# Both parts of a weight unit in one tile, 64 bytes beside a multiple of 128

## The chip, the cores and the metric

The kernel runs on one core of a Trainium2 chip. The metric is the device time of one execution in microseconds (us). Before the change it is 2307.37 us, the median of 3 runs (2305.29 to 2307.74).

## What is computed

Two transformer blocks in sequence, both on one sequence of 256 tokens of width 1024, all in float32. The first has two layers: a mixer (an mLSTM group with neighbourhood attention in the one, differential attention in the other), cross attention to 256 memory tokens, and a SwiGLU network with 2816 hidden units. The second has two layers of a SwiGLU network, a mixer of three gated branches (sparse latent attention with a top-64 choice, stick-breaking attention, a short convolution), cross attention, and another SwiGLU network. After each sublayer stands a layer norm over a scaled residual:

```python
def swiglu(x, w_gu, w_down):
    gate, up = jnp.split(x @ w_gu, 2, axis=-1)
    return (jax.nn.silu(gate) * up) @ w_down
...
    x = layer_norm(DEEPNORM_ALPHA * x + ff, ln_g[layer, 2], ln_b[layer, 2])
```

With 256 tokens, nearly all arithmetic is in products of the activations with weight matrices, each weight being used once. The differential attention needs one scalar that the change touches:

```python
    lam = jnp.exp(jnp.sum(lp[0] * lp[1])) - jnp.exp(jnp.sum(lp[2] * lp[3])) + lam_init
    ...
        a = p[:, :, 0] - lam * p[:, :, 1]
```

## The kernel before

**Weight units.** Every weight matrix is cut on the host into units of 128 partitions x 1024 columns of float32 (512 KB), 725 of them (the memory tokens are cut in the same way). The class Stream (line 190) holds the list of units in the order of their use, recorded by a first pass over the program without instructions. Its method _load (line 203) starts a unit's transfer into one of 4 staging tiles `w`, on SyncE's queue. Its method _split (line 211) makes two tiles of it: `hi`, the unit rounded to fp32r by ScalarE (L218), and `lo`, what the rounding left out, by VectorE (L219; put off by `due`, so that it is issued a little later, by `_low`). Up to 10 units are held split at a time, each part in one of the 10 places of its tag in the pool `wp`. pump (line 233) runs loads and splits ahead of use; get (line 248) hands a unit out, and done gives its place free.

**Products.** Activations are split in the same way: `xT` (hi and lo, feature by token), or `ph` and `pl` for computed operands. A float32 product is then three fp32r matmuls added up in PSUM: hi x hi, lo x hi, hi x lo. In unit_group (line 339) the weights are the stationary operand, in slices of 128 columns, and xT streams with 256 columns (L348, L350, L352: 3232 of each). mm3 (line 304, its matmuls L307 to L309) is used by all others: bg_mm, where a unit of the down or output projection streams with 512 or 256 columns against stationary `ph` and `pl`; vproj and vproj_first, where a unit streams with 512 columns against slices of xT; the first two units of each SwiGLU network; the branch products of the mixer; and in mem_open kv_k and kv_v, where both operands are units: the memory tokens, two units held through the whole of it, and the weights. Only the gates of the mLSTM (e_g) have a stationary operand of 64 columns.

**Order.** Instructions are issued in the order of the program, each engine has its own queue, and waits between engines follow from which tile places are written and read. Attention and other small work is written as generators (`bgs`), stepped between units by tick, so that TensorE does it between units. Small products there (L727, L747, L965, L1354 and others) are of plain float32, and the transposes (L551, L646) too; their operands lie in the pools `a1` (places of 1,024 bytes) and `a2` (its widest tile, `av`, is 128 x 4 x 129 float32, 2,064 bytes, and places are kept at multiples of 32 bytes). The pools follow one another in a partition's memory: `one`, `stage`, `wp`, `a1`, `a2` and two small ones.

**Lambda.** tables (line 1466) computes minus lambda for all partitions: a subtraction of the two exponentials, a subtraction of lambda's constant, and a matmul with a row of ones (`onerow`), which spreads it over 128 partitions. build sets `onerow` and `negone` (a 128 x 128 tile of -1, used by the stick-breaking attention) by memsets at the start.

Of the kernel before, what the change touches and what calls it, by code (L numbers as in the profile page):

```python
# [9 lines left out]
F32 = mybir.dt.float32  # L10
F32R = mybir.dt.float32r
AF = mybir.ActivationFunctionType
OP = mybir.AluOpType
# [8 lines left out]
LAM_INIT = 0.8 - 0.6 * math.exp(-0.3)  # L22
# [145 lines left out]

class Blank:


# [16 lines left out]
class Stream:  # L190
# [20 lines left out]
    def _split(self):  # L211
        n = self.net
        cols = self.plan[self.split][2]
        w = self.stage.pop(self.split)
        hi = n.wp.tile([128, 1024], F32R, tag="wh", name="wh")
        lo = n.wp.tile([128, 1024], F32R, tag="wl", name="wl")
        self._low()
        n.nc.scalar.copy(hi[:, :cols], w[:, :cols])  # L218
        self.due = lambda: n.nc.vector.tensor_sub(lo[:, :cols], w[:, :cols], hi[:, :cols].bitcast(F32))  # L219
        self.parts[self.split] = (hi, lo)  # L220
        self.split += 1
        self.live += 1
# [44 lines left out]
class Net:  # L267
# [1198 lines left out]
    def tables(self):  # L1466
        nc, sg, nlam, lp = self.nc, self.sg, self.nlam, self.lp
        nc.vector.tensor_scalar(sg, sg, 1.0 - LAM_INIT, None, op0=OP.mult)

        l2 = self.small.tile([1, 2], F32, tag="l2", name="l2")  # L1470
        pr = self.k1(shape=[1, 64], name="lpr")
        for i in range(2):
            nc.vector.tensor_mul(pr, lp[:, 128 * i:128 * i + 64], lp[:, 128 * i + 64:128 * i + 128])
            nc.vector.reduce_sum(l2[:, i:i + 1], pr, axis=AX.X)
        nc.scalar.activation(l2, l2, AF.Exp)
        nl = self.small.tile([1, 1], F32, tag="l1", name="l1")
        nc.vector.tensor_sub(nl, l2[:, 1:2], l2[:, 0:1])
        nc.vector.tensor_scalar(nl, nl, LAM_INIT, None, op0=OP.subtract)
        for _ in range(4):
            yield  # L1480
        self.rel_table()
        ps = self.bank([128, 1])
        nc.tensor.matmul(ps, self.onerow, nl, start=True, stop=True)
        nc.vector.tensor_copy(nlam, ps)

    def rel_load(self):
# [7 lines left out]
    def build(self):  # L1494
        nc, tc = self.nc, self.tc
        with ExitStack() as ctx:
            pool = lambda name, bufs, **k: ctx.enter_context(tc.tile_pool(name=name, bufs=bufs, **k))
            self.one = pool("one", 1)
            self.stage = pool("stage", STAGE)
            self.wp = pool("wp", W_SLOTS)  # L1500
            self.act = Multi(pool("a1", 35), pool("a2", 18)) if self.real else Blank()
            self.small = SmallMix(pool("sm_col", 24), pool("sm_o", 2)) if self.real else Blank()
            self.psum = pool("psum", 8, space=bass.MemoryType.PSUM)
            self.dram = pool("dram", 1, space=bass.MemoryType.DRAM)
            ctx.enter_context(tc.manual_schedule())
            sq = self.one.tile([128, 3, 128], F32, name="sq")
            self.xT = [self.one.tile([128, 8, S], F32R, tag=f"xT{i}", name="xT") for i in range(2)]
            xq = [self.k2(name="xq") for _ in range(4)]
            for u in range(4):
                nc.scalar.dma_start(xq[u], self.a["xT"][u // 2, :, (u % 2) * 512:(u % 2) * 512 + 512]  # L1510
                                    .rearrange("p (k c) -> p k c", k=2))
            self.xq = xq
            self.ws.start()
            nc.sync.dma_start(sq, self.a["c_sq"])
            self.ident, self.negt, self.strict = (sq[:, i, :] for i in range(3))
            self.mhalf = self.one.tile([128, 8], F32, name="mhalf")
            nc.vector.memset(self.mhalf, -0.5)
            self.negone = self.one.tile([128, 128], F32, name="negone")
            nc.vector.memset(self.negone, -1.0)
            self.onerow = self.one.tile([1, 128], F32, name="onerow")  # L1520
            nc.vector.memset(self.onerow, 1.0)

            subs = [self.even,
                    lambda: self.xattn("x0", "memT", 2, 1),
                    lambda: self.ffn("f0", 2, 2 * ALPHA, 4 * EPS),
                    self.odd,
                    lambda: self.xattn("x1", "memT", 2, 4),
                    lambda: self.ffn("f1", 5, 2 * ALPHA, 4 * EPS)]
            for l in range(2):
                b = 6 + 4 * l  # L1530
                subs += [lambda l=l, b=b: self.ffn(f"h{l}0", b, 4 * ALPHA, 16 * EPS),
                         lambda l=l, b=b: self.mixer(l, b + 1),
                         lambda l=l, b=b: self.xattn(f"y{l}", "memT2", 1, b + 2),
                         lambda l=l, b=b: self.ffn(f"h{l}1", b + 3, 4 * ALPHA, 16 * EPS)]
            if self.start:
                for u in range(4):
                    self.x_split(u)
                self.late_loads()
                self.lam_load()
                self.rel_load()  # L1540
                for _ in self.tables():
                    pass
            for f in subs[self.start:self.stop]:
                f()
            if self.stop < 14:
                self.flush()
                for t in range(2):
                    nc.sync.dma_start(self.out[0, t * 128:t * 128 + 128, :], self.x[:, t, :])
# [40 lines left out]
```

## Time and profile before

| | before |
|---|---|
| median of 3 runs | 2307.37 us |
| profiled execution's own time | 2310.04 us |
| its span | 2308.3 us |
| TensorE (PE) busy | 2277.5 us |
| weight loads (PEld) busy | 2139.0 us |
| VectorE (DVE) busy | 1498.5 us |
| ScalarE (ACT) busy | 1156.3 us |
| GpSimd (POOL) busy | 201.9 us |
| moved from HBM | 403.76 MB, 175 GB/s over the span |
| granted TensorE clock, mean | 0.996 |

Busy times are unions: a matmul's recorded duration of some 0.28 us runs from its start to the modelled end of its way through the array, and several overlap, so that the distance from one start to the next tells the pace and not the duration. A weight load (PEld) runs beside the matmul before its own. Names such as `wh` and `wl` are the program's tiles, with numbers left out; L218 is line 218 of the kernel.

### The profile page before, as it was taken

The numbers are of one execution on the slowest core, as the hardware profiler recorded it, in microseconds if no ns is written. First come the engines' busy times: TensorE is split into PE (matmuls) and PEld (weight loads), VectorE is DVE, ScalarE is ACT, GpSimd is POOL, SyncE is SP. The second block draws the span as 40 slices with busy tenths as digits, with TensorE's granted clock in tenths as the row PEclk, the third lists the DMA queues.
The fourth block names the chain that finished last, engine by engine and source line by source line (L and its number), as shares of the span: only waits on it lengthen the run. The fifth ranks groups of instructions, "written<-read, shape, count | busy, mean of one in ns | idle before, by whom it ended". The sixth has DMA issues, their size and how long they took to land.

```text
span 2308.3 us, 40983 instructions
## 1 busy us (share of the span) xinstructions
PE 2277.5 (99%) x16600; PEld 2139.0 (93%) x16600; DVE 1498.5 (65%) x2271; ACT 1156.3 (50%) x1856; POOL 201.9 (9%) x239
## 2 busy tenths in 40 slices
PE   8999999999999999999999999999999999999998
PEld 6989999998999999999899999999999999999998
DVE  4885665676657557556586677557656576677655
ACT  5555454377435444444745554444443845445542
POOL 0720000011000000000202000000000101100000
PEclk9999999999999999999999999999999999999999
DMA  7644475463437555654364555654753445454752
GB/s 232 164 165 165 158 249 183 146 210 138 161 131 248 183 182 179 207 182 159 116 188 142 202 174 191 210 191 138 238 191 130 165 150 170 162 195 163 248 183 74
DMA packets 118081, 407.50 MB, mean 177 GB/s; under 512 B 14169, under 2 KB 19419, under 8 KB 117891
## 3 DMA queue, kind: packets, MB, share of 16 engines
q1 hardware_dynamic: 116258, 402.00, 52.2%
q0 software_dynamic: 768, 1.57, 0.8%
q8 instruction: 130, 2.13, 0.4%
q10 hardware_dynamic: 864, 1.31, 0.2%
q14 instruction: 61, 0.49, 0.1%
HBM read 403.76 MB, written 1.06 MB: 175 GB/s over the span
## 4 chain that ended last, share of the span: by engine, by line
PE 95%; ACT 2%; DVE 2%; DMA 1%; POOL 0%; issue 0%; ACTq 0%; DVEq 0%; POOLq 0%
PE ps L348 17%; PE ps L350 16%; PE ps L352 16%; PE acc L307 7%; PE acc L308 7%; PE acc L309 7%; PE ps L307 5%; PE ps L309 5%; PE ps L308 5%; PE ps L551 1%; PE ps L727 1%; PE ps L747 1%; DMA xq<-in_xT 1%; PE ps L646 1%; DVE x L536 0%; PE ps L1145 0%
## 5 line engine op out<-in xcount | busy, mean ns | idle before, releaser
L219 DVE TENSOR_TENSOR wl<-w,wh 128x1024 fp32r<-128x1024 f32 x725 | 884.3, 1239 | 378.0 <-ACT wh L218 374.9
L348 PE MATMUL ps<-xT,wh 128*128 128x256 f32 x3232 | 921.5, 285 | 0.0
L350 PE MATMUL ps<-xT,wl 128*128 128x256 f32 x3232 | 914.6, 283 | 0.0
L352 PE MATMUL ps<-xT,wh 128*128 128x256 f32 x3232 | 914.3, 283 | 0.0
L218 ACT CAST wh<-w 128x1024 fp32r<-128x1024 f32 x725 | 747.5, 1050 | 233.3 <-PE ps L352 134.6
L348 PEld LDWEIGHTS ps<-xT,wh 128*128 128x128 f32 x3232 | 619.8, 192 | 10.0 <-issue 5.5
L350 PEld LDWEIGHTS ps<-xT,wl 128*128 128x128 f32 x3232 | 620.0, 192 | 0.6
L352 PEld LDWEIGHTS ps<-xT,wh 128*128 128x128 f32 x3232 | 620.0, 192 | 0.0
L307 PE MATMUL acc<-wh,ph 128*128 128x512 f32 (+1 forms) x940 | 329.2, 350 | 0.6 <-ACT ph L295 0.6
L308 PE MATMUL acc<-wl,ph 128*128 128x512 f32 (+1 forms) x940 | 327.2, 348 | 0.0
L309 PE MATMUL acc<-wh,pl 128*128 128x512 f32 (+1 forms) x940 | 326.0, 347 | 0.0
L307 PEld LDWEIGHTS acc<-wh,ph 128*128 128x128 f32 x940 | 177.9, 189 | 24.9 <-ACT ph L295 0.8
L309 PEld LDWEIGHTS acc<-wh,pl 128*128 128x128 f32 x940 | 177.5, 189 | 23.2 <-DVE pl L296 0.2
L308 PEld LDWEIGHTS acc<-wl,ph 128*128 128x128 f32 x940 | 178.0, 189 | 22.3
L522 POOL TENSOR_TENSOR col<-col,mhalf 128x1 f32<-128x1 f32 (+1 forms) x38 | 28.6, 752 | 1596.7 <-DVE col L530 1521.4
L563 ACT ACTIVATE k<-ps 128x256 f32<-128x256 f32 x120 | 46.0, 383 | 179.2 <-PE ps L352 179.2
L292 ACT CAST ph<-k 128x256 fp32r<-128x256 f32 x120 | 48.8, 407 | 128.7 <-DVE k L565 128.7
L307 PE MATMUL ps<-wh,xT 128*128 128x256 f32 (+1 forms) x304 | 103.9, 342 | 9.4 <-ACT wh L218 9.4
L307 PE MATMUL ps<-wh 128*128 128x256 f32 x384 | 112.6, 293 | 0.0
L564 DVE SCALAR_TENSOR_TENSOR k<-k,ps 128x256 f32<-128x256 f32 x120 | 50.4, 420 | 93.9 <-ACT k L563 93.8
L309 PE MATMUL ps<-wh,wl 128*128 128x256 f32 x384 | 108.6, 283 | 0.0
L308 PE MATMUL ps<-wl,wh 128*128 128x256 f32 x384 | 108.5, 282 | 0.0
(266 smaller groups left out, 2502.1 us busy)
## 6 DMA issues: line engine op xcount, KB each, us to landing
w<-in_h_g SPq DMA_DIRECT2D x160, 512.0 KB, 4.2
w<-in_h_d SPq DMA_DIRECT2D x88, 512.0 KB, 4.2
w<-in_f_g SPq DMA_DIRECT2D x80, 512.0 KB, 4.2
w<-in_m_gate SPq DMA_DIRECT2D x48, 512.0 KB, 3.7
w<-in_f_d SPq DMA_DIRECT2D x44, 512.0 KB, 4.2
gb<-in_ln_row SPq DMA_DIRECT2D x28, 512.0 KB, 6.8
w<-in_m_c SPq DMA_DIRECT2D x24, 512.0 KB, 3.2
w<-in_m_br SPq DMA_DIRECT2D x24, 512.0 KB, 3.3
```

Source lines behind the costliest of these rows:

```text
L218: n.nc.scalar.copy(hi[:, :cols], w[:, :cols])
L219: self.due = lambda: n.nc.vector.tensor_sub(lo[:, :cols], w[:, :cols], hi[:, :cols].bitcast(F32))
L292: nc.scalar.copy(hi, src)
L307: mm(ps, a[0], b[0], start=first, stop=False)
L308: mm(ps, a[0], b[1], start=False, stop=False)
L309: mm(ps, a[1], b[0], start=False, stop=last)
L348: mm(ps, ws[i][0][:, k, :], xh[:, k, :], start=k == 0, stop=False)
L350: mm(ps, ws[i][1][:, k, :], xh[:, k, :], start=False, stop=False)
L352: mm(ps, ws[i][0][:, k, :], xl[:, k, :], start=False, stop=k == 7)
L522: self.nc.gpsimd.tensor_tensor(y, v, self.mhalf[:, :n], op=OP.pow)
L563: nc.scalar.activation(h, pg, AF.Tanh, scale=0.5)
L564: nc.vector.scalar_tensor_tensor(h, in0=h, scalar=1.0, in1=pg, op0=OP.add, op1=OP.mult)
```

## The change

hi and lo of a unit become slices of one tile `w2` of 2,048 + 32 columns (8,320 bytes): the first 16 columns are left empty, hi has the next 1,024, lo the 1,024 after it, and the last 16 are empty again. The pool `wp` has 10 places of 8,320 bytes in place of 10 of 4,096 for each part. The row of ones goes, 512 bytes of the pool `one`; lambda is computed with its own sign and spread by a row of `negone`, which turns it.

```diff
+HALF = 16
...
     def _split(self):
         n = self.net
         cols = self.plan[self.split][2]
         w = self.stage.pop(self.split)
-        hi = n.wp.tile([128, 1024], F32R, tag="wh", name="wh")
-        lo = n.wp.tile([128, 1024], F32R, tag="wl", name="wl")
+        both = n.wp.tile([128, 2048 + 2 * HALF], F32R, tag="w2", name="w2")
+        hi, lo = both[:, HALF:HALF + 1024], both[:, HALF + 1024:HALF + 2048]
         self._low()
         n.nc.scalar.copy(hi[:, :cols], w[:, :cols])
         self.due = lambda: n.nc.vector.tensor_sub(lo[:, :cols], w[:, :cols], hi[:, :cols].bitcast(F32))
...
         nl = self.small.tile([1, 1], F32, tag="l1", name="l1")
-        nc.vector.tensor_sub(nl, l2[:, 1:2], l2[:, 0:1])
-        nc.vector.tensor_scalar(nl, nl, LAM_INIT, None, op0=OP.subtract)
+        nc.vector.tensor_sub(nl, l2[:, 0:1], l2[:, 1:2])
+        nc.vector.tensor_scalar(nl, nl, LAM_INIT, None, op0=OP.add)
         for _ in range(4):
             yield
         self.rel_table()
         ps = self.bank([128, 1])
-        nc.tensor.matmul(ps, self.onerow, nl, start=True, stop=True)
+        nc.tensor.matmul(ps, self.negone[0:1, :], nl, start=True, stop=True)
         nc.vector.tensor_copy(nlam, ps)
...
-            self.onerow = self.one.tile([1, 128], F32, name="onerow")
-            nc.vector.memset(self.onerow, 1.0)
```

## Rows read from the trace of the kernel before

**Rows 1.** The page: busy us of each engine, share of the span, instructions.

```profile
PE 2277.5 (99%) x16600; PEld 2139.0 (93%) x16600; DVE 1498.5 (65%) x2271; ACT 1156.3 (50%) x1856; POOL 201.9 (9%) x239
```

**Rows 2.** Groups of TensorE instructions by form: count, busy us, mean ns, idle before.

```profile
L348 PE MATMUL ps<-xT,wh 128*128 128x256 f32 x3232 | 921.5, 285 | 0.0
...
L307 PE MATMUL acc<-wh,ph 128*128 128x512 f32 x564 | 222.7, 395 | 0.6 <-ACT ph L295 0.6
...
L307 PE MATMUL ps<-wh 128*128 128x256 f32 x384 | 112.6, 293 | 0.0
...
L307 PE MATMUL acc<-wh,ph 128*128 128x256 f32 x376 | 106.6, 283 | 0.0
...
L307 PE MATMUL ps<-wh,xT 128*128 128x256 f32 x192 | 56.9, 297 | 0.0
...
L307 PE MATMUL ps<-ph,wh 128*128 128x256 f32 x192 | 56.8, 296 | 0.0
...
L307 PE MATMUL ps<-wh,xT 128*128 128x512 f32 x112 | 47.0, 420 | 9.4 <-ACT wh L218 9.4
```

**Rows 3.** TensorE in order of time (start, duration us), streamed 256-column units, 19 matmuls.

```profile
1001.79 0.28 PE L348 MATMUL ps<-xT,wh 128*128 128x256 f32 x1
...
1003.95 0.28 PE L348 MATMUL ps<-xT,wh 128*128 128x256 f32 x1
```

**Rows 4.** TensorE in order of time, down projection, 512 columns, 16 matmuls.

```profile
2289.05 0.39 PE L307 MATMUL acc<-wh,ph 128*128 128x512 f32 x1
...
2292.45 0.39 PE L307 MATMUL acc<-wh,ph 128*128 128x512 f32 x1
```

**Rows 5.** Tile wl: weight loads of 64 columns, durations min/median/max, first and last start.

```profile
L309 PE MATMUL ps<-xT,wl x16: 276/276/277, 28.4 to 33.5; 128*64 128x256 f32 x16
```

**Rows 6.** Two stretches: us, PE busy (instructions), granted clock, DMA share, GB/s.

```profile
19.00:25.50 6.50, 5.97 (x13) 0.50 0.91 317
...
1271.00:1315.00 44.00, 44.00 (x369) 1.00 0.53 174
```

**Rows 7.** TensorE in order of time at the lower clock, 10 matmuls.

```profile
21.35 0.63 PE L307 MATMUL ps<-wh,xT 128*128 128x512 f32 x1
...
25.19 0.60 PE L307 MATMUL ps<-wh,xT 128*128 128x512 f32 x1
```

**Rows 8.** One matmul each at 220.66, 238.20, 657.82 and 1222.51 us: groups by form.

```profile
L309 PE MATMUL ps<-wh,wl 128*128 128x256 f32 x1 | 0.3, 281 | 0.0
...
L309 PE MATMUL ps<-wh,wl 128*128 128x256 f32 x1 | 0.3, 283 | 0.0
...
L309 PE MATMUL ps<-wh,wl 128*128 128x256 f32 x1 | 0.3, 279 | 0.0
...
L352 PE MATMUL ps<-xT,wh 128*128 128x256 f32 x1 | 0.3, 286 | 0.0
```

**Rows 9.** All engines in order of time: halves of tile x, and its transposes.

```profile
2107.16 0.42 PEld L551 LDWEIGHTS ps<-sq,x 128*128 128x128 f32 x4 [0.38 <-POOL x L538]
...
2108.49 1.26 POOL L538 TENSOR_TENSOR x<-x,gb 128x512 f32<-128x512 f32 x1 [1.38 <-ACT x L537]
```

**Rows 10.** TensorE's waits: us in total, times, longest us.

```profile
PE ps L307 <- ACT wh L218: 9.4, 2, 7.0
...
PE ps L308 <- DVE wl L219: 1.7, 3, 0.8
```

**Rows 11.** VectorE in order of time at the start.

```profile
1.05 0.17 DVE L1521 MEMSET onerow<- 1x128 f32 x1
...
6.05 0.69 DVE L293 TENSOR_TENSOR xT<-xq,xT 128x512 fp32r<-128x512 f32 x1 [4.84 <-ACT xT L292]
```

**Rows 12.** Groups of VectorE instructions by form.

```profile
L219 DVE TENSOR_TENSOR wl<-w,wh 128x1024 fp32r<-128x1024 f32 x725 | 884.3, 1239 | 378.0 <-ACT wh L218 374.9
...
L293 DVE TENSOR_TENSOR xT<-ps,xT 128x512 fp32r<-128x512 f32 x52 | 35.9, 690 | 32.6 <-ACT xT L292 32.5
...
L517 DVE SCALAR_TENSOR_TENSOR x<-x,acc 128x512 f32<-128x512 f32 x42 | 28.6, 681 | 46.8 <-PE acc L309 46.8
```

## The prediction

> **What bounds the kernel now.** I read the busy shares first: TensorE is busy 2277.5 us of the 2308.3 us span, VectorE 65%, ScalarE 50% [rows 1]. So the time is TensorE's, and only two things can move it: how far apart its matmuls start, and the little time in which it waits. Next the groups by form, for the counts [rows 2]. Each row is one of the three products of a split pair, so a unit's matmuls are three times its row. With 256 columns against a 128-column load that is 3 x (3232 + 384 + 376 + 192 + 192) = 13,128; with 512 columns 3 x (564 + 112) = 2028; and 48 with a 64-column load [rows 5]. Then the order of time, for the spacing. The streamed units start 0.120 us apart: (1003.95 - 1001.79) / 18 [rows 3]. The 512-column ones start 0.2267 us apart: (2292.45 - 2289.05) / 15 [rows 4]. Together 13,128 x 0.1200 = 1575 us and 2028 x 0.2267 = 460 us, 2035 us with the 5 of the small ones left out.
>
> What the columns alone need can be read at the lower clock. From 19 to 25.5 us the granted clock is 0.50 (1.2 GHz), and 512-column matmuls start (25.19 - 21.35) / 9 = 0.4267 us apart, 1.2 columns per ns [rows 6, 7]. At 2.4 GHz, the level of the steady stretch [rows 6], that is 106.7 ns for 256 and 213.3 for 512 columns. The measured 120.0 and 226.7 are both 13.3 ns longer. With a 64-column load the spacing is (33.5 - 28.4) / 45 = 113.3 ns, 6.7 longer [rows 5]. So each 128-column weight load takes 13.3 ns from the matmul beside which it runs, in proportion to its columns, and only at the full clock. Over 13,128 + 2028 = 15,156 matmuls this is 202 us. It is the only large thing that an address could touch: an operand is read for the load while another streams for the matmul.
>
> **The change, part by part.**
>
> *The 64 bytes.* By the program's allocation every stationary and moving operand of these matmuls (hi, lo, xT, ph, pl) now starts 128 bytes past a multiple of 256. After the change a unit's place is 8,320 bytes, 32.5 x 256, so hi and lo start at 192 and at 64 past 256 in turn; xT stays where it is, and ph and pl move by 768 bytes, 3 x 256. All slices are multiples of 512 bytes. So one operand of nearly every matmul shifts by 64 bytes against the other; in the memory products of kv_k and kv_v both shift.
>
> No row shows an fp32r load at such a place. The nearest are the loads that follow a unit's last matmul from the act pool, whose places lie 2,080 bytes apart (the widest tile, av, has 2,064). A matmul's recorded duration follows its loss: 283 ns is the regular one [rows 2], 276 goes with the 64-column load [rows 5], 7 ns less as the spacing is 6.7 less. Of the four single matmuls [rows 8] the one beside a load at 192 past 256 took 281, at 64 past 256 283, at 32 279, and beside a transpose's load at 160 286. None comes near the 270 that it would take without the loss. The two places which the change uses give -2 and 0 ns; the best and worst of any place -4 and +3. Taken for 15,156 matmuls: -1 ns each (half the units at either place) is -15 us, -4 is -61, +3 is +45. But these are single loads, of plain fp32, at the end of a stream, and a stream may settle otherwise. A matmul whose two reads come at a fixed rate of two to one passes through every relative position during a load, which is why I expect the loss to be the same wherever they start. I take 0, and keep -61 and +45 as ends.
>
> Rule of the Trainium skill: "SBUF — State Buffer", section "Who interferes with whom", gives TensorE two independent read ports, one for the moving operand and one for the weight load, and says that it waits for nobody. By that rule no place of an operand changes anything, the spacing would be the columns alone and this change would be worth exactly 0. The trace disagrees on the spacing: 120.0 against 106.7 ns. So there is something that a change could gain, and the rule can't be leaned on to exclude it.
>
> *One tile for both parts.* ScalarE still writes hi and VectorE lo, now in one tile. If waits went by whole tiles, the first matmul of a unit would wait for lo too. They go by regions: the transposes of the first half of x start at 2107.16, while the add that writes the second half of the same tile, earlier in the program, starts at 2108.49 [rows 9]. So 0. Were it otherwise, it would cost only where a unit is late: TensorE waits for hi 9.4 us in two places and for lo 1.7 us in three [rows 10], so at most five times the 1.24 us of the subtraction [rows 12], +6 us. A place is handed out again when both parts are free; hi is read by the last product, so hi sets it today as well. 0.
>
> *ScalarE and VectorE on shifted tiles.* The nearest rows are 512 elements on xT (128 past 256, 690 ns) and on x (32 past a multiple of 128, 681 ns) [rows 12]: -1%. On the subtraction's 1239 ns this is -16 ns, and VectorE waits 374.9 us for ScalarE before it in any case [rows 12]. 0 from both sides, hidden beside TensorE's matmuls.
>
> *Lambda and the constant.* The two tiny operations keep their number and form, with signs turned. The matmul reads a row of -1 in place of +1. One 0.17 us memset goes; VectorE is idle 4.84 us behind it [rows 11]. 0.
>
> Sum: 0 on the profiled execution's 2310.04 us (span 2308.3 and 1.7 around it), which lies 2.7 us above the median of the three runs, 2307.37. I forecast 2307 us, 2303 to 2312.
>
> **Rivals.**
>
> *The stream finds a better position (faster).* In a steady stream each load starts with a matmul, so a fixed shift of the two reads could avoid collisions that a single load can't. For it: the loss is a matter of two reads at once, since at 1.2 GHz it is nil [rows 7], and the duration does move with the place, 279 to 286 [rows 8]. Against it: the two places in question gave 281 and 283. Price: from -1 ns (2292 us) by way of -4 ns (2246 us) to half the loss, -6.7 ns x 15,156 = -101 us, 2206 us.
>
> *The stream finds a worse one (slower).* Same place, TensorE's spacing. It decides from about +0.3 ns a matmul, 5 us. For it: 286 at one place [rows 8], and 395 ns as the mean of the 512-column products [rows 2], longer than the 0.39 us of the steady ones [rows 4], so a load can take more than 13.3 ns. Half the units at +3 ns gives +23 us, 2330 us; all of them +45, 2353 us.
>
> *Whole-tile waits after all:* +6 us, 2313 us.
>
> *It doesn't do what it says:* were the places rounded to another step, the units would lie as before: 2307 us. I count it with no change.
>
> **How the numbers follow.** No change 0.37, the unmade change among it; better position 0.36, worse position 0.25, whole-tile waits 0.02. Of the better position I give two thirds to 2230 us or more; of the worse, four fifths to less than 2340. So 2230 to 2340 leaves out 0.12 below and 0.05 above. About 0.2% (4.6 us) is what a measurement of this kernel can tell from no change: faster 0.36, same 0.37, slower 0.27.
>
> **What would show it.** The spacing of the streamed units: 0.120 us if I am right, less or more otherwise, and the same number read as L348's mean duration (285 now). If the loss goes, the weight load's duration beside it should change too. If only every second unit changes, it is the place past 256; if all do, the multiple of 128. Kv_k, both of whose operands shift, should stay as it is in every case; if it changes with the others, it is the place itself and not the distance. TensorE's waits for hi and lo should stay at 9.4 and 1.7 us. The prediction is wrong if the spacing moves by more than 0.3 ns, or if TensorE is no longer busy to 99%.

## The result and the profile after

| | kernel before | changed kernel |
|---|---|---|
| median of the runs, us | 2307.28 (2305.29 to 2307.74, 4 runs) | 2267.69 (2266.29 to 2268.32, 4 runs) |
| ratio to before, 95% interval | | 0.9829 [0.9813, 0.9844] |
| profiled execution: own time / span, us | 2310.04 / 2308.3 | 2266.29 / 2264.6 |

The change is 39.6 us faster, 1.7%. The forecast was no change; the time lies inside its range, and is what the first rival, the better position, was to bring.

The page after: busy time of each engine as in [rows 1], the granted clock in 40 slices of the span, and of its costliest groups VectorE's subtraction and a weight load of the streamed units:

```profile
PE 2231.1 (99%) x16600; PEld 2086.4 (92%) x16600; DVE 1496.6 (66%) x2270; ACT 1155.1 (51%) x1856; POOL 202.3 (9%) x239
...
PEclk9999999999999999999999999999999999999999
...
L222 DVE TENSOR_TENSOR w<-w,w 128x1024 fp32r<-128x1024 f32 x725 | 882.6, 1238 | 367.4 <-ACT w L221 363.5
...
L351 PEld LDWEIGHTS ps<-xT,w 128*128 128x128 f32 x3232 | 607.9, 188 | 10.0 <-issue 5.5
```

TensorE is the bound as before. Its busy time is 46.4 us less, its instructions are as many, and the granted clock is at 90% of full speed or more in all 40 slices of either page (the line PEclk reads the same before). So the matmuls start closer together. The groups by form that answer to [rows 2]:

```profile
L351 PE MATMUL ps<-xT,w 128*128 128x256 f32 x3232 | 906.6, 281 | 0.0
...
L310 PE MATMUL acc<-w,ph 128*128 128x512 f32 x564 | 223.2, 396 | 0.6 <-ACT ph L298 0.6
...
L310 PE MATMUL ps<-w,w 128*128 128x256 f32 x384 | 112.4, 293 | 0.0
...
L310 PE MATMUL acc<-w,ph 128*128 128x256 f32 x376 | 105.9, 282 | 0.0
```

The streamed units' mean went from 285 to 281 ns, the memory products (both operands shifted) kept 293, and the 512-column products got slightly longer, 395 to 396. The order of time shows what is behind the 281. Two stretches of streamed units, 45 and 47 intervals:

```profile
344.28 0.28 PE L351 MATMUL ps<-xT,w 128*128 128x256 f32 x1
...
349.58 0.28 PE L351 MATMUL ps<-xT,w 128*128 128x256 f32 x1
...
352.73 0.28 PE L351 MATMUL ps<-xT,w 128*128 128x256 f32 x1
...
358.06 0.28 PE L355 MATMUL ps<-xT,w 128*128 128x256 f32 x1
```

The first goes at (349.58 - 344.28) / 45 = 117.8 ns, the second at (358.06 - 352.73) / 47 = 113.4 ns; before, every unit went at 120.0 [rows 3]. Over the whole trace, taking the second half of each of the 404 units, 187 run at 113.3 ns and 217 at 117.8, none at 120.0. A unit keeps its pace from its first few products on, and of the 183 units that follow another unit directly, 170 have the pace of the one before. Which units lie at 64 past a multiple of 256 and which at 192 can be told from the 32-byte kernel below, where the two kinds run at different paces: of the 203 at 64, 81 have the lower pace here, of the 201 at 192, 106 (means 116.0 and 115.4 ns).

Adding up the intervals from one matmul's start to the next (those up to 0.3 us; longer ones are waits) gives where the 43.7 us between the two spans come from:

| products | count | before, us | after, us | difference |
|---|---|---|---|---|
| streamed units and the gate unit, 256 columns | 9744 | 1176.2 | 1136.1 | -40.1 |
| background, 512 columns (weights streamed) | 1692 | 384.2 | 388.7 | +4.5 |
| x loaded, weights streamed, 512 columns | 336 | 68.2 | 71.5 | +3.3 |
| background, 256 columns | 1128 | 133.9 | 130.8 | -3.1 |
| branch and x loaded, 256 columns | 1152 | 144.8 | 138.5 | -6.3 |
| memory products, 256 columns | 1152 | 139.1 | 138.4 | -0.7 |
| everything else, waits included | | 247.2 | 245.9 | -1.3 |

(Of the third row's +3.3, 2.3 are ten intervals that were over 0.3 us before and stood with the waits; the others went from 228.2 to 231.5 ns on the mean, 1.1 us for 336. In the profiled execution before, the granted clock was 0.50 from 19 to 25.5 us [rows 6]; in the one after it was 1.00 there. The ten intervals, 0.2 us longer for it, are some 2 us of why the spans differ by 43.7 us and the medians by 39.6. The 48 products of the gate unit, with loads of 64 columns, became slower, from 113.5 to 119.1 ns.)

TensorE's waits for the two halves of a weight unit, which answer to [rows 10]:

```profile
PE ps L310 <- ACT w L221: 9.0, 3, 7.0
...
PE ps L311 <- DVE w L222: 2.7, 4, 0.8
```

9.0 and 2.7 us against 9.4 and 1.7: nothing of the gain is there, and one tile for both halves makes no unit late.

### The profile page after: what moved, and what is told of

The parts are those of the page before. It is cut to its first block, busy times and chain, and to the rows that moved or that the text cites. A ratio compares the mean times of both kernels' runs of the same rounds, so it can differ in the third digit from the quotient of the medians.

```text
span 2264.6 us, 40982 instructions
## 1 busy us (share of the span) xinstructions
PE 2231.1 (99%) x16600; PEld 2086.4 (92%) x16600; DVE 1496.6 (66%) x2270; ACT 1155.1 (51%) x1856; POOL 202.3 (9%) x239
## 4 chain that ended last, share of the span: by engine, by line
PE 90%; DVE 3%; ACT 3%; DMA 2%; issue 1%; POOL 1%; SPq 0%; DVEq 0%; ACTq 0%; POOLq 0%
PE ps L351 15%; PE ps L353 15%; PE ps L355 15%; PE acc L312 7%; PE acc L310 7%; PE acc L311 7%; PE ps L310 5%; PE ps L312 5%; PE ps L311 5%; DVE w L222 1%; ACT w L221 1%; PE ps L554 1%; PE ps L730 1%; PE ps L750 1%; DMA w<-in_o_qk 1%
## 5 line engine op out<-in xcount | busy, mean ns | idle before, releaser
L222 DVE TENSOR_TENSOR w<-w,w 128x1024 fp32r<-128x1024 f32 x725 | 882.6, 1238 | 367.4 <-ACT w L221 363.5
L351 PE MATMUL ps<-xT,w 128*128 128x256 f32 x3232 | 906.6, 281 | 0.0
L353 PE MATMUL ps<-xT,w 128*128 128x256 f32 x3232 | 899.5, 278 | 0.0
L355 PE MATMUL ps<-xT,w 128*128 128x256 f32 x3232 | 899.3, 278 | 0.0
L221 ACT CAST w<-w 128x1024 fp32r<-128x1024 f32 x725 | 747.9, 1050 | 229.8 <-PE ps L355 124.7
L351 PEld LDWEIGHTS ps<-xT,w 128*128 128x128 f32 x3232 | 607.9, 188 | 10.0 <-issue 5.5
L353 PEld LDWEIGHTS ps<-xT,w 128*128 128x128 f32 x3232 | 607.9, 188 | 0.6
L355 PEld LDWEIGHTS ps<-xT,w 128*128 128x128 f32 x3232 | 606.9, 188 | 0.0
L310 PE MATMUL acc<-w,ph 128*128 128x512 f32 (+1 forms) x940 | 329.1, 350 | 0.6 <-ACT ph L298 0.6
L312 PE MATMUL acc<-w,pl 128*128 128x512 f32 (+1 forms) x940 | 327.3, 348 | 0.0
L311 PE MATMUL acc<-w,ph 128*128 128x512 f32 (+1 forms) x940 | 326.4, 347 | 0.0
L310 PEld LDWEIGHTS acc<-w,ph 128*128 128x128 f32 x940 | 176.7, 188 | 25.6 <-ACT ph L298 0.8
L311 PEld LDWEIGHTS acc<-w,ph 128*128 128x128 f32 x940 | 176.7, 188 | 25.3
L312 PEld LDWEIGHTS acc<-w,pl 128*128 128x128 f32 x940 | 176.5, 188 | 24.2 <-DVE pl L299 0.2
L310 PE MATMUL ps<-w,w 128*128 128x256 f32 x384 | 112.4, 293 | 0.0
L310 PE MATMUL ps<-w,xT 128*128 128x256 f32 (+1 forms) x304 | 101.1, 333 | 9.0 <-ACT w L221 9.0
L312 PE MATMUL ps<-w,w 128*128 128x256 f32 x384 | 108.3, 282 | 0.0
L311 PE MATMUL ps<-w,w 128*128 128x256 f32 x384 | 108.1, 282 | 0.0
```

Source lines behind the costliest of these rows:

```text
L310: mm(ps, a[0], b[0], start=first, stop=False)
L311: mm(ps, a[0], b[1], start=False, stop=False)
L312: mm(ps, a[1], b[0], start=False, stop=last)
L351: mm(ps, ws[i][0][:, k, :], xh[:, k, :], start=k == 0, stop=False)
L353: mm(ps, ws[i][1][:, k, :], xh[:, k, :], start=False, stop=False)
L355: mm(ps, ws[i][0][:, k, :], xl[:, k, :], start=False, stop=k == 7)
```

## The experiments

In what follows, the *distance* is the place of the streamed operand less the place of the operand loaded beside it, modulo 256 bytes. Before, it was 0 nearly everywhere. The changed kernel's weights lie at 64 and 192 in turn and x at 128, so its units have distances +64 and -64. The theory was that this distance sets the pace; its rivals were the one tile, the place of the weights by itself, and what ran just before.

**One tile, no 64 bytes.** Is it the one tile, or the address?

```
-        hi, lo = both[:, HALF:HALF + 1024], both[:, HALF + 1024:HALF + 2048]
+        hi, lo = both[:, 0:0 + 1024], both[:, 0 + 1024:0 + 2048]
```

> The change with hi and lo still in one tile of 8,320 bytes, lambda and the constant as changed, but the slices start at the tile's start: hi and lo lie at a multiple of 128 again, a multiple of 128 away from xT, ph and pl. Theory (the gain is the 64 bytes between the two reads of TensorE, and one tile is worth nothing): streamed units back at 120.0 ns, 512-column products back at 227 ns, 2307 us (within 5). Rival (one tile and its fewer places and waits bring the gain): 2268 us. Rival (the distance matters modulo 256; odd places now lie 128 bytes off): half the units below 120 ns, about 2285 us.

2306.01 us, ratio 0.9993 [0.9984, 1.0002]. The tile, the waits by region and the lambda edit are worth nothing that the time shows. Half of the units now lie 128 bytes from x; those run at 118.7 ns on the mean, the others at 120.0. So the rival of the distance modulo 256 had the kind right, but not the size: the units gain 5.7 us by their intervals, and the 512-column products, of which half lie 128 bytes off as well, lose 3.4 us in the background alone.

**The 64 bytes, two tiles.** A 64-byte pad ahead of the weights and one behind them (weights at 192, the split parts `ph` and `pl` of the activations at 0):

```
+            pool("pad0", 1).tile([128, 16], F32, name="pad0")
             self.wp = pool("wp", W_SLOTS)
+            pool("pad1", 1).tile([128, 16], F32, name="pad1")
```

> The kernel before, two tiles, lambda and constant unchanged; only a 64-byte tile stands ahead of the pool wp and one behind it, so that all units lie 64 bytes beside a multiple of 128 and everything behind them at a multiple of 128. Theory (distance of the reads): the same pace as the change, streamed units 113 to 118 ns, 2268 us (within 8, as which of the two paces a unit falls into depends on what came before it). Rival (one tile brings it): 2307 us.

2269.17 us, ratio 0.9836 [0.9821, 0.985]: the address alone brings the change's gain. 217 units at 113.3 ns, 187 at 117.8. Its groups by form:

```profile
L348 PE MATMUL ps<-xT,wh 128*128 128x256 f32 x3232 | 907.6, 281 | 0.0
...
L307 PE MATMUL acc<-wh,ph 128*128 128x512 f32 x564 | 224.3, 398 | 0.6 <-ACT ph L295 0.6
```

**Roles.** The changed kernel, in which units that stream against a loaded operand, and the memory, go back to offset 0, while the loaded units stay 64 bytes beside:

```
-        cols = self.plan[self.split][2]
+        name, _, cols = self.plan[self.split]
...
+        at = 0 if name.endswith(("_d", "_o", "memT", "memT2", "_bv", "_av", "_ao", "_sv")) or name == "o_v" else HALF
...
-        hi, lo = both[:, HALF:HALF + 1024], both[:, HALF + 1024:HALF + 2048]
+        hi, lo = both[:, at:at + 1024], both[:, at + 1024:at + 2048]
```

> The change, but units that stream with 512 columns (down and output projections, e_bv, e_av, e_ao, o_v, sv) and the memory tokens stay at a multiple of 128; all others lie 64 bytes beside. Theory (distance of the two reads counts, not the place): 512-column products back from about 231 to 227 to 229 ns (2028 of them, -6 us), kv_k and kv_v from 120 to 116 ns (1,152, -5 us), the 256-column part of the output projections from 117 back to 120 (1,128, +3 us): 2260 us, 2253 to 2268. Rival (the place of the units alone counts): kv stays at 120 ns, and the products whose units are moved back lose what they had: 2270 to 2275 us.

2260.3 us, ratio 0.9795 [0.9778, 0.9811]. In the memory products both operands had shifted alike in the changed kernel and kept 293 and 282 ns; now that they stand apart the groups by form read:

```profile
L311 PE MATMUL ps<-w,w 128*128 128x256 f32 x384 | 111.2, 290 | 0.0
...
L312 PE MATMUL ps<-w,w 128*128 128x256 f32 x384 | 106.9, 278 | 0.0
```

So it is the distance. The total came out as forecast, but not by the forecast parts. The 512-column products of the background were to come back to 227 to 229 ns and stayed at 231.2 on the mean, since they now lie at distances 0 and 128 in turn; the memory products gained 3.0 us of the 5 forecast; and the streamed units, for which nothing was forecast, gained 6.7 us, as 249 of them run at 113.3 ns here and 187 in the changed kernel.

**32 bytes.** The changed kernel with its slices at 8 columns in place of 16 (`both[:, 8:8 + 1024], both[:, 8 + 1024:8 + 2048]`).

> The change with the slices 32 bytes beside a multiple of 128 in place of 64. Theory (the two reads collide by position modulo 128, 64 being farthest): part of the gain, streamed units between 116 and 120 ns, 2268 to 2305 us. Rival (only whether the two lie in the same half of 128 bytes counts): 2300 to 2307 us, since most pairs of positions stay in the same halves as often. Rival (any place off a multiple of 128 will do): 2268 us or less.

2305.24 us, ratio 0.9991 [0.9982, 1.0001]. The distances are now -32 and +96: 118.3 and 119.9 ns. Units gain 8.3 us by their sum and the 512-column products lose as much (7.7 in the background alone): almost nothing is left. Not every displacement helps. The time lies just outside the range of the theory that 64 bytes is farthest modulo 128, and inside that of the rival that counts halves of 128 bytes. The runs below leave neither: x at +64 and at -64 is the same modulo 128, with 117.8 and 113.3 ns; and with x at +112 both operands start in the same half of 128 bytes, as at distance 0, and the units settle at 113.3 ns and not at 120.0.

**x alone, to either side.** The kernel before, where only the two x-transposed tiles move, to 192 or to 64 past 256 (pads of 16 and 48 columns around them, or 48 and 16):

```
+            self.one.tile([128, 16], F32, name="pad0")
             self.xT = [self.one.tile([128, 8, S], F32R, tag=f"xT{i}", name="xT") for i in range(2)]
+            self.one.tile([128, 48], F32, name="pad1")
```

> The kernel before (two tiles per unit at a multiple of 128), in which only the two tiles of x-transposed move, from a place at 128 past a multiple of 256 to one at 192; weights and split parts stay. Distance theory (what counts is how far the streamed operand lies from the weights loaded beside it, not where either lies): the 9,696 products of the streamed units and L219-type gate units fall from 120.0 ns to 113.3 or 117.9 ns each, -65 us if all settle at the lower pace, -20 us if all at the upper, about -42 us if they mix as before: 2242 to 2287, middle 2264 us. The 512-column background products (split part loaded, weights streamed, distance unchanged) stay at 227 ns and the kv products at 120, unlike in the changed kernel. Place theory (a weight tile off the multiple of 128 is read more cheaply): units stay at 120.0 ns, time 2307 us within 0.2%.

> As xT_192, but the tiles of x-transposed lie at 64 past a multiple of 256, 64 bytes to the other side of the weights. Distance theory, only the size of the distance counts: the same pace mix and the same time as xT_192 within 0.3%. If the side counts (what the unit takes over from the matmul before it differs by side): another share of units at 113.3 ns than in xT_192, and a time up to 45 us away from it, still between 2242 and 2287 us. Place theory: 2307 us.

At +64: 2287.4 us, ratio 0.9908 [0.9894, 0.9923]; 391 of 404 units at 117.8 ns, so the upper end of what was expected. At -64: 2253.22 us, ratio 0.9765 [0.9748, 0.9781]; 352 units at 113.3 ns. The weights did not move, and the side is worth 34 us. The place of the weights can't be the cause. Streamed units at +64 in the order of time, 47 intervals of (1007.93 - 1002.39) / 47 = 117.9 ns:

```profile
1002.39 0.28 PE L348 MATMUL ps<-xT,wh 128*128 128x256 f32 x1
...
1007.93 0.28 PE L352 MATMUL ps<-xT,wh 128*128 128x256 f32 x1
```

and at -64, from the first product after background products at distance 0:

```profile
1004.20 0.29 PE L348 MATMUL ps<-xT,wh 128*128 128x256 f32 x1
1004.33 0.28 PE L350 MATMUL ps<-xT,wl 128*128 128x256 f32 x1
1004.45 0.28 PE L352 MATMUL ps<-xT,wh 128*128 128x256 f32 x1
1004.56 0.28 PE L348 MATMUL ps<-xT,wh 128*128 128x256 f32 x1
...
1009.55 0.28 PE L352 MATMUL ps<-xT,wh 128*128 128x256 f32 x1
```

The first two intervals are 0.13 and 0.12 us (121 ns each by the trace's nanoseconds), the third 0.11 (116); the 44 that follow take (1009.55 - 1004.56) / 44 = 113.4 ns. A stream needs some products until it goes at its lower pace.

**Everything moved together.** 64 bytes ahead of all pools:

```
+            pool("pad0", 1).tile([128, 16], F32, name="pad0")
             self.one = pool("one", 1)
```

> The kernel before with 64 bytes set aside ahead of all its tiles, so that every operand of every matmul moves by 64 bytes together and all distances stay. Distance theory: unit pace stays at 120.0 ns, time 2307 us within 0.2%. Place theory: as the changed kernel, 2268 us.

2308.79 us, ratio 1.0002 [0.9992, 1.0011]; the group keeps its mean, and the units that no wait interrupts all run at 120.0 ns:

```profile
L348 PE MATMUL ps<-xT,wh 128*128 128x256 f32 x3232 | 921.4, 285 | 0.0
```

**The pattern by itself.** This is not the kernel: after a start of 240 products it runs, for each distance, a first unit at a set distance and two units at the distance under test, then the same with 512 columns; the rest is left out.

```
            for k in ks:
                wh, wl = (t[:, base + 128 * k:base + 128 * k + 128] for t in w)
                xh, xl = (t[:, base + o + S * k:base + o + S * k + S] for t in z)
                mm(ps[:, :S], wh, xh, start=first and k == ks[0], stop=False)
                mm(ps[:, :S], wl, xh, start=False, stop=False)
                mm(ps[:, :S], wh, xl, start=False, stop=last and k == ks[-1])
```

> Not the kernel, but the matmul pattern of a streamed unit by itself (24 products of 256 columns, weight tiles loaded in turn, high and low parts as in the kernel; everything else is left out and zeros are written). Per block 24 products with the streamed operand at a first distance (0, 192 or 64 bytes past the weights), then 48 at the distance under test, 0 to 240 bytes in steps of 16; all of it once with the weights at 128 past a multiple of 256 and once at 192; then 12 and 24 products of 512 columns likewise, with the weights streamed. Theory (the distance from loaded to streamed operand, with its sign, decides, and where both lie does not): 120.0 ns at 0; 113.3 ns at 192 (64 bytes below, as xT_64); 117.9 ns at 64 (as xT_192); 118 to 119 ns at 32 and 128, 119.9 ns at 160; the same table for both places of the weights. Rival (what ran just before decides between 113.3 and 117.9 ns, the sign only through it): the tables after the three first distances differ, with 113.3 ns at 64 too after some of them. No forecast for the distances that no kernel had; below 113.3 ns at any of them would mean that more than half of the loss can be had back. Streams of 512 columns: 227 ns at 0, 231 to 233 ns at 64, 128 and 192. Time of the run: 2,880 plus 6,912 products at 0.113 to 0.120 us less those of 512 columns, about 1.1 ms.

One execution, 1119.35 us. Pace of the last products of each block, in ns; the columns say at which distance the 24 products before it ran and at what pace they ended.

| distance | after 0 (120.0) | after -64 (113.4) | after +64 (117.7) | 512 columns, after 0 |
|---|---|---|---|---|
| 0 | 120.0 | 120.0 | 120.0 | 226.7 |
| +16 / -16 | 118.7 / 117.2 | 116.7 / 117.0 | 116.7 / 117.1 | 226.7 / 226.7 |
| +32 / -32 | 117.7 / 118.3 | 116.7 / 118.2 | 116.7 / 118.0 | 233.3 / 233.3 |
| +48 / -48 | 118.3 / 119.3 | 118.3 / 119.5 | 118.3 / 119.5 | 231 to 232 / 233.3 |
| +64 / -64 | 117.8 / 113.3 | 117.8 / 113.3 | 113.3 / 117.8 | 228.8 / 233.3 |
| +80 / -80 | 120.0 / 119.2 | 118.3 / 119.2 | 120.0 / 119.2 | 230.0 / 232.1 |
| +96 / -96 | 119.9 / 117.3 | 120.0 / 117.3 | 120.1 / 117.3 | 233.3 / 233.8 |
| +112 / -112 | 113.3 / 118.7 | 113.3 / 118.7 | 113.3 / 116.7 | 226.7 / 233.3 |
| 128 | 118.7 | 118.7 | 118.7 | 232.6 |

(The paces of the first units have exceptions: the unit at -64 ran at 117.8 ns ahead of the blocks at 0 and +32, the unit at +64 at 113.3 to 113.4 ahead of those at +32 to +80.) With both operands 64 bytes further on, the table is the same to 0.1 ns. In the order of time, 47 intervals each (46 in the first pair): +64 after a first unit at 0; -64 after 0; +64 after a first unit at +64 that itself ran at 113.4; -64 after a first unit at +64:

```profile
75.94 0.28 PE L48 MATMUL ps<-z,w 128*128 128x256 f32 x1
...
81.36 0.28 PE L46 MATMUL ps<-z,w 128*128 128x256 f32 x1
...
144.24 0.29 PE L46 MATMUL ps<-z,w 128*128 128x256 f32 x1
...
149.58 0.28 PE L48 MATMUL ps<-z,w 128*128 128x256 f32 x1
...
346.18 0.28 PE L46 MATMUL ps<-z,w 128*128 128x256 f32 x1
...
351.51 0.28 PE L48 MATMUL ps<-z,w 128*128 128x256 f32 x1
...
413.74 0.28 PE L46 MATMUL ps<-z,w 128*128 128x256 f32 x1
...
419.27 0.28 PE L48 MATMUL ps<-z,w 128*128 128x256 f32 x1
```

117.8, 113.6, 113.4 and 117.7 ns. Both theories hold a part. At ten of the 16 distances the three columns agree within 0.3 ns, so the distance with its sign sets the pace; at +64 and -64 two paces 4.5 ns apart are possible, at +16, +32, +80 and -112 two that are 1 to 2 ns apart, and what ran before picks one. The paces that the expectation gave for 32 and 160 bytes came from the 32-byte kernel, whose distances it read with the wrong sign; put at -32 and +96, its 118.3 and 119.9 ns are the table's. For 512 columns the forecast held at 0, -64 and 128 and missed at +64 (228.8). There, too, what ran before can count: at +112 the stream takes 226.7 ns after a stream at 0, and 233.3 after one at +64. No distance went below 113.3.

**Gap.** The least edit that makes all units -64 and leaves the background at 0: 64 bytes between the held tiles and the rest.

```
             self.one = pool("one", 1)
+            pool("pad0", 1).tile([128, 16], F32, name="pad0")
             self.stage = pool("stage", STAGE)
```

> The kernel before with 64 bytes set aside behind the tiles that are held from the start (x-transposed among them) and ahead of the stage, the weights and the split parts: weights and split parts move together to 192 past a multiple of 256, x-transposed stays at 128. So x-transposed lies 64 bytes below the weights, as in xT_64, and the background products keep distance 0. Theory (signed distance and what ran just before; the places themselves don't count): the time and the paces of xT_64, 2253 us within 0.3%, some 350 of 404 units at 113.3 ns. Rival (in xT_64 it was the place of x-transposed, 64 past 256, that helped): x-transposed lies where it lay before, so 2307 us, or the 2269 us of the kernel with two tiles and pads, whose weights lie at the same place.

2253.61 us, ratio 0.9761 [0.9745, 0.9778]; 355 units at 113.3 ns. The groups by form:

```profile
L348 PE MATMUL ps<-xT,wh 128*128 128x256 f32 x3232 | 903.1, 279 | 0.0
...
L307 PE MATMUL acc<-wh,ph 128*128 128x512 f32 x564 | 221.7, 393 | 0.6 <-ACT ph L295 0.6
```

It differs from the kernel with two pads only in the place of the split parts, so in the background (and in that of the staging tiles, which TensorE doesn't read): the units have the same distance in both, but 355 against 217 of them find the lower pace. That is the effect of what ran before, in the kernel itself.

**Split parts alone.** 64 bytes ahead of the pool of the split parts (`pool("pad0", 1).tile(...)` before `self.act = ...`): units at 0, background at -64.

> The kernel before in which only the split parts (and what lies behind them) move by 64 bytes, so that the units keep distance 0 and 120.0 ns, while the weights that stream in the background products lie 64 bytes below the split parts loaded beside them. By the scan: 1,692 products of 512 columns go from 227 to 229 ns, +4 us; the 1,128 of 256 columns in the background, if they settle like units, from 120 to 113.3 ns, -7.5 us, if they don't, 0; the 576 branch products (64 bytes above) to 117.9 ns, -1 us: 2302 to 2310 us. If the streams of 512 columns go to the 233 ns that the changed kernel shows: +10 us, 2309 to 2316 us.

2311.98 us, ratio 1.002 [1.0011, 1.003], slower by 4.7 us. The lower of the two forecasts had again read the table with the wrong sign; the higher one holds, as the table has it for -64. 512-column products in the down projection, 16 intervals of (2291.63 - 2287.89) / 16 = 233.8 ns, or 233.3 by the trace's nanoseconds, against 226.7 in [rows 4]:

```profile
2287.89 0.40 PE L309 MATMUL acc<-wh,pl 128*128 128x512 f32 x1
...
2291.63 0.40 PE L307 MATMUL acc<-wh,ph 128*128 128x512 f32 x1
```

The background's 512 columns cost 7.8 us more, its 256 columns 2.8 less.

**x at +112.** The distance whose pace depended least on what came before:

```
-            self.xT = [self.one.tile([128, 8, S], F32R, tag=f"xT{i}", name="xT") for i in range(2)]
+            xt = [self.one.tile([128, 8 * S + 64], F32R, tag=f"xT{i}", name="xT") for i in range(2)]
+            self.xT = [t[:, 28:28 + 8 * S].rearrange("p (k s) -> p k s", k=8) for t in xt]
```

> The kernel before in which x-transposed lies 112 bytes above the weights (28 columns into a wider tile). In the scan this is the one distance that settled at 113.3 ns after all three first distances, but only after some 20 products at 115.4 ns. Theory (the scan holds in the kernel): units that follow another kind of product run at about 115.5 ns, units that follow a unit at 113.3 ns, none at 117.9 ns: mean 114 to 115 ns, 2249 to 2259 us. Rival (breaks between the units start the settling anew each time, or keep it out): 115.4 to 118 ns, 2262 to 2288 us.

2261.52 us, ratio 0.9797 [0.9783, 0.9812], just above the one range and just below the other. In their second halves 398 of 404 units run at 113.3 ns, as the theory has it, but a unit that follows another kind of product spends some eleven products at about 119:

```profile
1008.03 0.28 PE L348 MATMUL ps<-xT,wh 128*128 128x256 f32 x1
...
1009.34 0.28 PE L352 MATMUL ps<-xT,wh 128*128 128x256 f32 x1
...
1013.30 0.28 PE L350 MATMUL ps<-xT,wl 128*128 128x256 f32 x1
```

11 intervals of (1009.34 - 1008.03) / 11 = 119.1 ns, then 35 of (1013.30 - 1009.34) / 35 = 113.1; by the trace's nanoseconds 118.7 and 113.3. A unit has only 24 products, so a distance that settles in three (-64) beats one that settles in eleven. That is 2.6 us of the 9.8 between the spans of this kernel and the one with x at -64. The rest lies outside the units: by the intervals the branch products and those that load x cost 4.4 us more here, the 512 columns of the background 1.3, and the waits and small products 1.4.

## Why the prediction was right, and where it failed

**What bounds the kernel: right.** TensorE stays busy to 99%, and only the interval between matmul starts changed. That 13.3 ns beside each load could be touched by an address is what the runs show; the changed kernel's span is shorter by 43.7 us of the 202.

**The 64 bytes, taken as 0: this step failed.** By the prediction's own sign, a spacing that moves by more than 0.3 ns, the forecast of no change was wrong: the spacing of the units fell from 120.0 to 113.3 and 117.8 ns. The time lies in the range only because the range was drawn to take in both rivals. The 0 had two grounds.

The first was the single matmuls of [rows 8]: 281 and 283 ns beside loads at the two places, so -2 and 0. They sampled the wrong moment. In the trace with x at -64 the first two products after a change of distance still take 121 ns, and only from the fourth on do they take 113.4. A single load at an unusual place, at the end of a stream at distance 0, is most like such a first product: the four were followed 119 to 122 ns later by the next start. (Those loads were of plain float32; a stream of them was not run.) The caveat that a stream may settle otherwise was the case that came.

The second was the thought that two reads at a fixed rate of two to one pass through every relative position, so that the start can't matter. It fell with the kernels in which x alone moved: 120.0 ns at 0, 117.8 at +64 and 113.3 at -64.

In its place: a stream at distance +64 or -64 loses 6.7 ns a product (113.3, half of the 13.3) or 11.1 (117.8), and keeps the one that it fell into. With 187 and 217 units in these two states the units gain 40.1 us with the gate unit, 4.1 ns for each of 9744 products. The middle price that the rival named, -4 ns, is the units' mean price, by luck: it was read from a single load at 32 bytes, and the mean is a mix of two paces. What the rival had wrong was to give it to all 15,156 matmuls. The 512-column ones went the other way, +2.7 ns (background) and +3.3 ns (x loaded), 5.6 us in all, as the table has it for a mix of +64 (228.8) and -64 (233.3). So the second rival, the stream that finds a worse position, happened too, in the same kernel.

**Where rule and trace were weighed.** "SBUF — State Buffer" of the Trainium skill, section "Who interferes with whom", gives TensorE separate ports for the two reads. By that the places of x and w would be of no account; the runs disagree, by 34 us between +64 and -64 with the same instructions. Setting the rule aside was right; the sum then came to the same 0 by way of single rows.

**One tile: right.** The kernel with one tile at offset 0 is the kernel before to within 0.2%, and the waits for hi and lo are 9.0 and 2.7 us.

**Shifted tiles on ScalarE and VectorE, lambda, memset: right in size.** Taken as 0 from both sides. VectorE's subtraction takes 1238 ns against 1239 [rows 12], and the one-tile kernel holds the lambda edit too.

**The signs.** Kv_k stayed, as forecast for every case (its operands now lie 0 or 128 bytes apart, and 0.7 us is what 120.0 and 118.7 ns in turn give), and moved when its operands were set 64 bytes apart: it is the distance, not the place. The weight load's duration went with the loss, 192 to 188 ns. "If all units change, it is the multiple of 128" was half right: units at both places gained (116.0 and 115.4 ns on the mean), but being off a multiple of 128 isn't enough, since at distance +96 the pace is 119.9, and at 128 it is 118.7 and not 120.0.

**The slower side** got 0.25 for a worse position. Its mechanism was real and the split parts moved alone show it (+4.7 us). That the units outweigh it was to be read from the counts, 9,744 against 2,028.

## What to carry to other kernels

Where TensorE is the bound and products of 256 columns stream against fresh weights, look at the interval between matmul starts, not at durations, and compare it with the columns at the granted clock; a constant excess is a price that the relative address of the two operands can change, here by half. A pad of 64 bytes that puts the streamed operand below the loaded one, with the 512-column products left at distance 0, was worth 2.4%, against 1.7% for the change itself, which shifted both kinds of product and put every second unit on the other side. Don't judge a steady stream by single instructions: leave out its first dozen, and take at least a dozen in a row after them.

## What the runs showed that was not expected

- The same code at the same addresses can run at two paces, 113.3 and 117.8 ns, from unit to unit. At a fixed distance of -64, 355 or 217 of 404 units have the lower one, as the background products ahead of them lie at distance 0 or -64. By which property of the earlier stream the pace is picked was not settled.
- The best pace leaves 6.7 ns of loss. None of the 16 distances, in steps of 16 bytes, gave less; steps below 16 bytes were not tried.
- The -64 that helps 256 columns most is among the worst for 512: these have their least, 226.7 ns, at 0, at 16 bytes to either side and, after a stream at 0, at +112, and take 228.8 to 233.8 elsewhere.
- Why a load costs time at one distance and half as much at another, the traces don't show.
